# A list-scheduling planner for a two-layer encoder: its DMA transfers served first in, first out, with new service times and tails

## The chip, the cores and the metric

The kernel runs on one core of a Trainium2 chip. The metric is device time in microseconds (us) of one execution. A core has five engines with in-order instruction queues: TensorE (PE in the rows, PEld for its weight loads), VectorE (DVE), ScalarE (ACT), GpSimd (POOL) and SyncE (SP). SP issues every transfer of this kernel; 16 DMA engines carry them.

## The reference, cut to what matters

A trunk of two layers runs over two groups of rows, x_prompt (512 x 1024) and x_sample (1024 x 1024), with shared weights:

```python
def even_layer(x, ...):                      # layer 0
    h = rms_norm(x, norm_g)
    qa, ka, va, qb, kb, vb, gate = split(h @ w_in)
    oa = gqa_attention(axial_rope(rms_norm(qa)), axial_rope(rms_norm(ka)), va)    # 8 query heads, 2 key heads
    ob = rms_norm(diff_attention(partial_rope(..qb), partial_rope(..kb), vb, lam)) * (1 - lambda_init)
    return x + (concat(oa, ob) * silu(gate)) @ w_out

def odd_layer(x, ...):                       # layer 1
    q, k, v, gate = split(rms_norm(x, norm_g) @ w_in)
    o = dilated_attention(q, k, v)           # 16 heads, patterns (128,1), (512,4), (2048,16), merged by softmax weights
    return x + (o * silu(gate)) @ w_out
```

Outputs are y_prompt and y_sample, in float32.

## The kernel before, in words

**Number format.** An operand of a matmul is held as two fp16 halves (high and low), and each product is made in three passes (PASSES: high x high, high x low, low x high).

**Units and granules.** The 1024 rows of w_in and w_out are handled in blocks of 128 output columns. Layer 0 has four units of grouped attention (A) and four of differential attention (B); layer 1 has eight dilated units (C). A unit works on three granules of 512 rows: gi 0 is the prompt, gi 1 and 2 are the sample. For a granule it projects keys and values (kv_piece), queries and gate (qg_piece), makes scores (tile S, L771, L1121, L1169, L1174), takes the exponential, splits the probabilities in two halves (tile h, L795 and L799), has them transposed by DMA (t<-h, L358), and multiplies them with the values (L783, called AV below: 24 or 48 small matmuls into a pj tile).

**The start.** Tiles of 128 rows of x are loaded (L1538), squared on ACT (L1544), scaled, and split into halves on ACT and DVE (h_split, L372 to L377). A DMA transpose of 2048 columns (L385) puts each into hT, from which all projections of the layer are made (L491). hT00 belongs to the prompt, hT01 to the sample (8 transposes). ACT also evicts projections from PSUM into tile z (L653, L732) and scales weights (L422, L472).

**Layer 1's merge.** In a C unit the third pattern's result (tile pk) goes to another layout by four small sends (pn<-pk, L1150), which POOL waits for at L1200.

**The order.** No engine's order is found on the chip. Class Plan is a list scheduler that runs in Python while the kernel is built: each stage has an engine, a duration, a priority pos, what it depends on, and buffers (tokens, limited by CAPS) that it acquires and gives back. run() simulates the engines by these durations. Whenever an engine is free it takes the ready stage with the lowest pos whose buffers are free, and emits its instructions then. A transfer is three stages: the issue on SP, a service on a single server called DMA, and a parallel tail on LAT; who depends on the transfer becomes ready after the tail. The durations never reach the chip; they only decide in which order the instructions stand.

```python
    def dma(self, issue, dur, fn, deps=(), acq=(), use=(), pos=None, keep=0, tail=1.0):
        a = self.add("SP", issue, fn, deps, acq, use, pos, keep)
        x = self.add("DMA", dur, None, [a], (), tuple(acq) + tuple(use), pos)
        return self.add("LAT", tail, None, [x], (), tuple(acq) + tuple(use), pos)
```

Of the kernel before, what the change touches and what calls it, by code (L numbers as in the profile page):

```python
# [59 lines left out]
class Plan:  # L60
# [24 lines left out]
    def dma(self, issue, dur, fn, deps=(), acq=(), use=(), pos=None, keep=0, tail=1.0):  # L85
# [6 lines left out]
    def tdma(self, cols, *args, **kw):  # L92

        return self.dma(0.05 + cols * 0.975e-3, cols * 1.45e-3, *args, tail=0.5, **kw)

# [110 lines left out]
T_DMA = 1.85  # L206
# [6 lines left out]
def trunk_kernel(ctx: ExitStack, tc: tile.TileContext, A: dict, outs: list):  # L213
# [77 lines left out]
    def norm_gain(l, deps=()):  # L291
# [9 lines left out]
        ld = dma(ISSUE, T_DMA, f_ld, deps, [tok])  # L301
# [96 lines left out]
    def wprep(w, cols, ih=None, iz=None, kinds=("whl",), deps=(), keep=2):  # L398
# [10 lines left out]
        for i, c0 in enumerate(cols):  # L409
# [5 lines left out]
            ld = dma(ISSUE, T_DMA, f_ld, deps, [rt], keep=keep)  # L415
# [100 lines left out]
    def qk_stages(zb, ztok, evs, e2, tabs, tdep, ti, kind, isq, dst, dst_acq, dst_use, swap, dst_dep=()):  # L516
# [81 lines left out]
        w1 = dma(ISSUE, 0.3, lambda: nc.sync.dma_start(out=swap()[0:64], in_=dst()[64:128]), [s], (), dst_use)  # L598
        w2 = dma(ISSUE, 0.3, lambda: nc.sync.dma_start(out=swap()[64:128], in_=dst()[0:64]), [s], (), dst_use)
# [23 lines left out]
    def kv_piece(u, gi):  # L623
# [4 lines left out]
        for hf in range(2):  # L628
# [44 lines left out]
            if u.kind == "C":  # L673
                for j in range(2):
# [10 lines left out]
                    vc = dma(ISSUE, 0.3, f_vc, [vl, u.vc_open], (), [u.vct[g], u.vtok])  # L685
# [125 lines left out]
    def spill(l, u, gi, dep):  # L811
# [5 lines left out]
        s = dma(ISSUE, 1.0, f, [dep], (), [u.sgtok[gi]])  # L817
# [87 lines left out]
    def att_B(u, gi):  # L905
# [15 lines left out]
        def chain(b, e0, e1, lo0, n, scs_, f4ts, ex, h4t, first):  # L921
# [9 lines left out]
            s = add("POOL", 0.66, f_co, [s], pos=P.pos - 20)  # L931
# [102 lines left out]
        def fin():  # L1034
# [5 lines left out]
            s = add("ACT", 1.1, f_sq, avs[-1:], (), [otok])  # L1040
# [24 lines left out]
    def att_C(u, gi):  # L1065
# [73 lines left out]
        def send():  # L1139
# [4 lines left out]
            s = add("ACT", act(512) + 0.12, f_ev, avs23[-1:], [pkt], [ot23])  # L1144
            ob["sent"] = []
            for j in range(4):
                def f(j=j):
# [46 lines left out]
        def fin():  # L1194
# [65 lines left out]
    def out_tile(l, g, tl, wo, mix_deps, x_deps, finish):  # L1260
# [264 lines left out]
    def l0_h(g, tls, kinds):  # L1525
# [4 lines left out]
        for i, tl in enumerate(tls):  # L1530
# [185 lines left out]
```

## Time and profile before

| | |
|---|---|
| time, median of 3 runs | 1867.0 us (1866.86 to 1868.43) |
| the profiled execution's own time | 1870.77 us |
| its span, first to last instruction | 1868.5 us |
| mean granted TensorE clock | 0.957 |
| PE / PEld busy | 1671.1 us (89%) / 1399.3 us (75%) |
| DVE / ACT / POOL busy | 1345.7 us (72%) / 1211.2 us (65%) / 692.3 us (37%) |
| instructions | 44772, of them 17626 matmuls |

2.3 us of the profiled execution lie outside its span, and it is 3.8 us above the median. Busy time is time in which an engine executes; PE's own idle time is the span less 1671.1 us, 197.4 us.

### The profile page before, as it was taken

The page shows a single profiled execution, that of the slowest core. Times are in us where ns is not written, and L with a number is a line of the kernel's source. Part 1 is how long each engine was busy: PE and PEld are TensorE (multiplying, and loading weights), DVE is VectorE, ACT ScalarE, POOL GpSimd, SP SyncE. Part 2 cuts the span into 40 slices and gives each one's busy share as a digit, 9 for nine tenths or more (in the row PEclk, how much of TensorE's full clock was granted, in tenths as well). Part 3 has the DMA queues.
Part 4 walks back from the last instruction along what each step waited for, and adds up shares of the span by engine and source line. Part 5 has one row for each costly group of instructions (what it writes and reads, how often), then busy time and mean ns, then how long its engine had stood idle before and what let it go on. Part 6 is the DMA issues. An engine that isn't in the chain of part 4 may idle for free.

```text
span 1868.5 us, 44772 instructions
## 1 busy us (share of the span) xinstructions
PE 1671.1 (89%) x17626; PEld 1399.3 (75%) x17626; DVE 1345.7 (72%) x2985; ACT 1211.2 (65%) x2593; POOL 692.3 (37%) x1204
## 2 busy tenths in 40 slices
PE   4598888999998999697899999999999999995998
PEld 3485676778787877476788887878788888874888
DVE  5779888877887878874555777777777777788442
ACT  5559787777776668753434777676767667787320
POOL 3533233343454453422222435353535353433200
PEclk9799999999999999898999999999999999997999
DMA  9778899987464456697985668586768576777993
GB/s 249 156 136 161 161 177 191 156 161 141 88 127 98 84 116 114 124 200 189 219 199 136 120 134 167 108 166 113 164 117 161 113 142 119 153 152 175 218 233 100
DMA packets 788724, 282.06 MB, mean 151 GB/s; under 512 B 647072, under 2 KB 772256, under 8 KB 788512
## 3 DMA queue, kind: packets, MB, share of 16 engines
q1 hardware_dynamic: 788512, 279.19, 72.7%
q8 instruction: 138, 2.26, 0.5%
q14 instruction: 74, 0.61, 0.1%
HBM read 73.92 MB, written 25.17 MB: 53 GB/s over the span
## 4 chain that ended last, share of the span: by engine, by line
PE 46%; DVE 10%; DMA 10%; POOL 6%; ACT 5%; issue 4%; SPq 0%; DVEq 0%; POOLq 0%; ACTq 0%
PE pj L491 35%; DMA t<-h 9%; PE pj L783 4%; PE pj L505 2%; PE S L1121 2%; DVE f L1096 2%; PE S L771 2%; POOL qs L260 1%; DVE h L799 1%; PE S L1169 1%; ACT f L1106 1%; DVE bs L1017 1%; DVE f L934 1%; ACT f L981 1%; DVE t L566 1%
## 5 line engine op out<-in xcount | busy, mean ns | idle before, releaser
L491 PE MATMUL pj<-whl,hT 128*128 128x256 f16 x7680 | 880.8, 275 | 27.3 <-DMA hT<-h 27.0
L491 PEld LDWEIGHTS <-hT 128*128 128x128 f16 x7968 | 780.2, 99 | 142.4 <-DMA hT<-h 31.3
L783 PEld LDWEIGHTS <-t 128*128 128x128 f16 x4992 | 203.5, 101 | 98.3 <-DMA t<-h 85.7
L1106 ACT ACTIVATE f<-f,cs,csc 128x256 f32<-128x256 f32 (+1 forms) x384 | 218.7, 573 | 82.2 <-DVE cs L777 82.1
L491 PEld LDWEIGHTS <-t 128*128 128x128 f16 x2304 | 228.7, 100 | 47.3 <-DMA t<-h 17.8
L799 DVE TENSOR_TENSOR h<-f,h 128x1024 f16<-128x1024 f32 x148 | 199.6, 1352 | 43.5 <-ACT h L795 43.2
L783 PE MATMUL pj<-V,t 128*128 128x64 f16 (+1 forms) x4032 | 180.4, 204 | 47.3 <-DMA t<-h 46.8
L771 PE MATMUL S<-K,q 128*128 128x512 f16 x640 | 168.9, 397 | 51.4 <-ACT f L1023 21.0
L491 PE MATMUL pj<-whl,t 128*128 128x256 f16 x1728 | 200.7, 278 | 15.7 <-DMA t<-h 13.9
L795 ACT ACTIVATE h<-f 128x1024 f16<-128x1024 f32 x168 | 175.8, 1052 | 14.8 <-DMA t<-h 12.5
L534 POOL TENSOR_SCALAR qs<-qs,we 128x8 f32<-128x8 f32 x87 | 43.0, 495 | 340.6 <-DVE qs L528 320.7
L260 POOL TENSOR_TENSOR qs<-qs,mhalf 128x8 f32<-128x8 f32 x87 | 147.6, 1696 | 7.3
L771 PEld LDWEIGHTS <-q 128*128 128x128 f16 x640 | 61.7, 101 | 109.4 <-issue 58.8
L1331 DVE SCALAR_TENSOR_TENSOR f<-pj,os,f 128x256 f32<-128x256 f32 x96 | 42.0, 479 | 108.9 <-PE pj L491 108.4
L853 DVE TENSOR_REDUCE as<-S 128x1 f32<-128x1024 f32 (+1 forms) x80 | 96.4, 1218 | 15.6 <-PE S L771 15.4
L863 ACT ACTIVATE f<-S,as,asc 128x1024 f32<-128x1024 f32 (+1 forms) x96 | 101.7, 1061 | 7.8 <-DVE h L799 4.4
L477 DVE SCALAR_TENSOR_TENSOR whl<-f,wsm,whl 128x1024 f16<-128x1024 f32 x68 | 94.3, 1400 | 6.4 <-ACT whl L472 6.3
L1096 DVE CUSTOM_DVE_ANT_0 f<-S,mask 128x256 f32<-128x256 f32 x192 | 69.7, 421 | 25.3 <-PE S L1169 25.3
L799 POOL TENSOR_TENSOR h<-f,h 128x1024 f16<-128x1024 f32 x20 | 43.4, 2172 | 117.3 <-ACT h L795 104.3
L422 ACT ACTIVATE t<-f 128x1024 bf16<-128x1024 f32 x74 | 77.8, 1052 | 14.0 <-DMA f<-in_w_in_dram 11.3
L1017 DVE TENSOR_REDUCE bs<-S 128x1 f32<-128x1024 f32 x64 | 76.9, 1217 | 13.2 <-PE S L771 13.2
L585 ACT ACTIVATE st<-t 128x512 f16<-128x512 f32 x87 | 54.2, 623 | 48.6 <-DVE t L579 32.1
(250 smaller groups left out, 2715.2 us busy)
## 6 DMA issues: line engine op xcount, KB each, us to landing
f<-in_w_in_dram SPq DMA_DIRECT2D x58, 512.0 KB, 5.4
mixbuf<-sg SPq DMA_DIRECT2D x48, 256.0 KB, 2.8
f<-mixbuf SPq DMA_DIRECT2D x24, 512.0 KB, 5.5
K<-K SPq DMA_DIRECT2D x78, 128.0 KB, 2.8
f<-in_w_out_dram SPq DMA_DIRECT2D x16, 512.0 KB, 5.1
pn<-pk SPq DMA_DIRECT2D x96, 66.0 KB, 2.6
x1buf<-f SPq DMA_DIRECT2D x12, 512.0 KB, 3.6
Vc<-V SPq DMA_DIRECT2D x96, 64.0 KB, 2.4
```

Of the source, the lines that this page charges most:

```text
L260: G.tensor_tensor(y, v, mhalf[:, 0:n], ALU.pow)
L477: stt(out=part(k, 1, i), in0=b[i][:, nk * k:nk * k + nk, :], scalar=sc(), in1=part(k, 0, i), op0=M, op1=SU)
L491: T.matmul(ps, lhs(k, a), wt(k, b), start=(k == 0 and i == 0), stop=(k == 7 and i == 2))
L771: T.matmul(out[:, 512 * i:512 * i + 512], q, u.K[:, st, gi, hk, :], start=(st == 0), stop=(st == 1))
L783: T.matmul(o, t4[:, 8 * a + base + k, :], v(k, b), start=(k == 0 and i == 0), stop=(k == nk - 1 and i == 2))
L795: S_.activation(out=b["hl"][:, 0, :], in_=b["e"], func=AF.Copy)
L799: (G if on_pool else V).tensor_tensor(b["hl"][:, 1, :], b["e"], b["hl"][:, 0, :], SU)
L853: V.tensor_reduce(out=b["s"][:, 0:nh], in_=b["S"].rearrange("p (h k) -> p h k", h=nh), op=ALU.max, axis=AX.X)
L863: S_.activation(out=b["e"][:, w * i:w * i + w], in_=b["S"][:, w * i:w * i + w], func=AF.Exp, bias=b["s"][:, 2 + i:3 + i], scale=u.sc, accu ...
L1017: V.tensor_reduce(out=b["s"][:, c:c + 1], in_=b["S", c], op=ALU.max, axis=AX.X)
L1096: V.tensor_tensor_reduce(out=b["e"][:, w * i:w * i + w], in0=b["S"][:, w * i:w * i + w], in1=mask(x), scale=1.0, scalar=-3.0e38, op0=AD, o ...
L1106: S_.activation(out=b["e"][:, w * i:w * i + w], in_=b["e"][:, w * i:w * i + w], func=AF.Exp, bias=b["s"][:, i:i + 1], scale=u.sc, accum_ou ...
```

## The change

Only the planner's rules and numbers change. The DMA server takes transfers in the order in which they become ready, no longer by pos. The service times become shorter and the tails longer: for a transpose of 2048 columns 2.97 + 0.5 us becomes 1.84 + 1.71 us, for a load 1.85 + 1.0 us becomes 1.3 + 1.9 us (rows) or 1.75 + 1.9 us (columns of a weight). Some stages of POOL and ACT get larger durations, and the four pn sends no longer depend on one another in the plan. Every line behind L203 moves down by one (by two between L1146 and L1152).

```diff
-    def dma(self, issue, dur, fn, deps=(), acq=(), use=(), pos=None, keep=0, tail=1.0):
+    def dma(self, issue, dur, fn, deps=(), acq=(), use=(), pos=None, keep=0, tail=1.25):
...
-        return self.dma(0.05 + cols * 0.975e-3, cols * 1.45e-3, *args, tail=0.5, **kw)
+        return self.dma(0.05 + cols * 0.975e-3, cols * 0.9e-3, *args, tail=1.2 + cols * 0.25e-3, **kw)
...
-                    heapq.heappush(engs[s.eng], (s.pos, s.seq, s))
+                    heapq.heappush(engs[s.eng], (t if s.eng == "DMA" else s.pos, s.seq, s))
...
-T_DMA = 1.85
+T_ROW = dict(dur=1.3, tail=1.9)
+T_COL = dict(dur=1.75, tail=1.9)
...
-            ld = dma(ISSUE, T_DMA, f_ld, (), [xts[i]])
+            ld = dma(ISSUE, fn=f_ld, acq=[xts[i]], **T_ROW)
...
-            ld = dma(ISSUE, T_DMA, f_ld, deps, [rt], keep=keep)
+            ld = dma(ISSUE, fn=f_ld, deps=deps, acq=[rt], keep=keep, **T_COL)
...
-        w1 = dma(ISSUE, 0.3, lambda: nc.sync.dma_start(out=swap()[0:64], in_=dst()[64:128]), [s], (), dst_use)
+        w1 = dma(ISSUE, 0.25, lambda: nc.sync.dma_start(out=swap()[0:64], in_=dst()[64:128]), [s], (), dst_use)
...
-        s = dma(ISSUE, 1.0, f, [dep], (), [u.sgtok[gi]])
+        s = dma(ISSUE, 0.6, f, [dep], (), [u.sgtok[gi]], tail=1.0)
...
-            s = add("ACT", 1.1, f_sq, avs[-1:], (), [otok])
+            s = add("ACT", 1.45, f_sq, avs[-1:], (), [otok])
...
-            s = add("POOL", 3.2 + pool(512), f_ch, [s, u.sg_ready[gi], u.cst], (), [u.sgtok[gi]])
+            s = add("POOL", 3.6 + pool(512), f_ch, [s, u.sg_ready[gi], u.cst], (), [u.sgtok[gi]])
...
+            s = add("NONE", 0.0, None, [s], [pnt])
...
-                ob["sent"].append(dma(ISSUE, 0.3, f, [s, ob["sent"][-1:]], [pnt] if j == 0 else (),
-                                      [pkt] + ([pnt] if j else [])))
+                ob["sent"].append(dma(ISSUE, 0.25, f, [s], (), [pkt, pnt]))
...
-            s = add("POOL", 1.0, f_w, [ob["sent"], avs1[-1:]], (), [pnt])
+            s = add("POOL", 1.4, f_w, [ob["sent"], avs1[-1:]], (), [pnt])
...
-            s = add("POOL", 0.55 + 3 * pool(512), f_p, [s, u.sg_ready[gi]], (), [pnt, u.sgtok[gi]])
+            s = add("POOL", 1.8 + 3 * pool(512), f_p, [s, u.sg_ready[gi]], (), [pnt, u.sgtok[gi]])
...
-        s = add("POOL", 2.0 + 0.15 * n, lambda: h_rms(b["s"], n), sqs)
+        s = add("POOL", 2.4 + 0.3 * n, lambda: h_rms(b["s"], n), sqs)
...
-        st = x1_done[g, tl] = dma(ISSUE, T_DMA, f_st, evs, (), [xt])
+        st = x1_done[g, tl] = dma(ISSUE, 1.05, f_st, evs, (), [xt], tail=1.6)
```

No instruction is added or taken away on any engine; what moves is the order. Three places show how.

ACT at the start of the program, where the prompt's first projections are evicted (z) while the sample's tiles are squared (L1544) and split (L377). Before:

```order
L653 ACTIVATE z0_280<-pj1_192 128x2x2x64
L661 ACTIVATE V1_282<-pj1_192 128x2x128
L653 ACTIVATE z0_280<-pj3_300 128x2x2x64
L661 ACTIVATE V1_282<-pj3_300 128x2x128
L523 ACTIVATE t11_382<-z0_280 128x512
L1544 ACTIVATE t10_427,hs4_174<-t41_113 128x1024
L1544 ACTIVATE t10_430,hs4_429<-t42_115 128x1024
L732 ACTIVATE z1_467<-pj0_355 128x2x2x64
L742 ACTIVATE sg0_474<-pj0_355,hz_475 128x256
L1544 ACTIVATE t10_478,hs4_429<-f42_172 128x1024
L1544 ACTIVATE t10_512,hs4_511<-f43_278 128x1024
L377 ACTIVATE h41_515<-t40_111 128x1024
```

The same rows of ACT's order after the change:

```order
L1545 ACTIVATE t11_246,hs4_227<-f42_181 128x1024
L1545 ACTIVATE t10_252,hs4_251<-f43_198 128x1024
L378 ACTIVATE h41_293<-t40_111 128x1024
L473 ACTIVATE whl1_296<-f40_158,wsm_188 128x8x128
L473 ACTIVATE whl1_296<-f41_170,wsm_188 128x8x128
L654 ACTIVATE z0_307<-pj1_201 128x2x2x64
L662 ACTIVATE V1_309<-pj1_201 128x2x128
L378 ACTIVATE h42_314<-t41_113 128x1024
L378 ACTIVATE h40_393<-t42_118 128x1024
L654 ACTIVATE z0_307<-pj3_316 128x2x2x64
L662 ACTIVATE V1_309<-pj3_316 128x2x128
L524 ACTIVATE t11_433<-z0_307 128x512
```

The squares and the first splits of the sample's tiles stand ahead of the evictions of z, or between them, where they stood behind.

SP, which issues the sample's loads and the transposes into hT01. Before, from the first such transpose's neighbourhood to the last:

```order
L1538 DMA t40_529<-in_x_sample_dram 128x1024
L385 DMA_TRANSPOSE hT01_534<-h41_515 128x16x128
L385 DMA_TRANSPOSE hT01_534<-h42_518 128x16x128
...
L385 DMA_TRANSPOSE hT01_534<-h41_556 128x16x128
L593 DMA_TRANSPOSE q0_678<-st1_634 128x8x128
L414 DMA f41_706<-in_w_in0_dram 128x8x128
L414 DMA f42_709<-in_w_in0_dram 128x8x128
L598 DMA K0_554<-K0_554 64x1024
L599 DMA K0_554<-K0_554 64x1024
L385 DMA_TRANSPOSE hT01_534<-h42_751 128x16x128
L385 DMA_TRANSPOSE hT01_534<-h40_768 128x16x128
```

SP after the change, the same stretch:

```order
L386 DMA_TRANSPOSE hT01_311<-h41_293 128x16x128
L1539 DMA t40_352<-in_x_sample_dram 128x1024
...
L386 DMA_TRANSPOSE hT01_311<-h42_314 128x16x128
L1539 DMA t42_443<-in_x_sample_dram 128x1024
L386 DMA_TRANSPOSE hT01_311<-h40_393 128x16x128
L386 DMA_TRANSPOSE hT01_311<-h41_441 128x16x128
...
L594 DMA_TRANSPOSE K0_598<-st0_569 128x8x128
L386 DMA_TRANSPOSE hT01_311<-h42_637 128x16x128
L386 DMA_TRANSPOSE hT01_311<-h40_640 128x16x128
...
L386 DMA_TRANSPOSE hT01_311<-h41_704 128x16x128
...
L386 DMA_TRANSPOSE hT01_311<-h42_716 128x16x128
L594 DMA_TRANSPOSE q0_803<-st1_762 128x8x128
```

The first sample transpose now stands ahead of the last three sample loads, and all eight stand ahead of the transpose of the first unit's q (L594, tile q0), behind which the last four stood.

PE at the end of layer 1, from the last unit's scores of granule 1 (q1) to the first block of the output projection (L491 with t); each row is the first of a group of like matmuls. Before:

```order
L1121 MATMUL S0_24990<-K1_23554,q1_24982 128x256
...
L1174 MATMUL S1_25083<-K1_23554,q1_24982 128x128
...
L783 MATMUL pj0_25150<-Vc2_24919,t42_25116 128x64
...
L783 MATMUL pj0_25150<-Vc2_24919,t40_25137 128x64
...
L1121 MATMUL S0_25223<-K1_23554,q2_25175 128x256
...
L783 MATMUL pj1_25267<-V0_23306,t41_25184 128x64
...
L1174 MATMUL S0_25293<-K1_23554,q2_25175 128x128
...
L783 MATMUL pj1_25267<-V0_23306,t42_25240 128x64
...
L1174 MATMUL S1_25351<-K1_23554,q2_25175 128x128
...
L783 MATMUL pj0_25396<-Vc2_24919,t40_25368 128x64
...
L491 MATMUL pj2_25445<-whl1_23799,t41_25383 128x256
```

After the change, the same place:

```order
L1122 MATMUL S0_25054<-K1_23553,q1_25014 128x256
...
L1175 MATMUL S1_25132<-K1_23553,q1_25014 128x128
...
L1122 MATMUL S0_25159<-K1_23553,q2_25097 128x256
...
L784 MATMUL pj2_25205<-Vc2_24928,t40_25174 128x64
...
L1175 MATMUL S0_25246<-K1_23553,q2_25097 128x128
...
L784 MATMUL pj2_25205<-Vc2_24928,t41_25243 128x64
...
L1175 MATMUL S1_25297<-K1_23553,q2_25097 128x128
...
L492 MATMUL pj1_25324<-whl1_24002,t42_25268 128x256
...
L784 MATMUL pj0_25399<-V0_23414,t41_25352 128x64
...
L492 MATMUL pj3_25429<-K0_24835,t42_25268 128x256
...
L784 MATMUL pj0_25399<-V0_23414,t41_25427 128x64
```

The first scores of granule 2 now stand ahead of the last AVs of granule 1, and blocks of the output projection stand between the AVs of granule 2.

## Rows read from the trace of the kernel before

**Rows 1.** Stretches of the span: length, busy PE, PEld, DVE, ACT, POOL, clock, DMA share, GB/s.

```profile
0.00:105.00 105.00, 58.39 (x403) 44.54 (x404) 66.88 (x129) 59.38 (x99) 43.06 (x76) 0.84 0.84 196
105.00:350.00 245.00, 212.00 (x2640) 166.02 (x2639) 205.61 (x277) 190.77 (x335) 90.44 (x105) 0.99 0.89 164
350.00:750.00 400.00, 383.26 (x3869) 314.81 (x3867) 322.56 (x522) 293.98 (x604) 175.10 (x313) 0.98 0.63 119
750.00:1000.00 250.00, 209.61 (x1822) 175.25 (x1819) 155.86 (x299) 125.67 (x216) 67.92 (x156) 0.91 0.82 188
1000.00:1650.00 650.00, 624.66 (x7060) 541.31 (x7061) 480.56 (x1444) 449.84 (x1147) 274.21 (x482) 0.98 0.68 135
1650.00:1760.00 110.00, 82.41 (x907) 67.58 (x906) 79.70 (x223) 73.42 (x172) 36.51 (x62) 0.84 0.85 185
...
53.62:99.91 46.29, 26.87 (x162) 18.91 (x162) 32.49 (x50) 27.16 (x49) 20.34 (x36) 0.71 0.86 181
...
1691.45:1729.73 38.28, 20.36 (x220) 15.02 (x220) 31.21 (x109) 31.86 (x80) 10.91 (x24) 0.63 0.85 185
```

**Rows 2.** Waits of PE, 0 to 105 us: line, releaser, us in total, times, longest.

```profile
PE pj L491 <- DMA hT<-h: 27.0, 8, 10.1
```

**Rows 3.** PE's timeline at the start: start, us, line, count, [idle before].

```profile
60.12 8.29 PE L491 MATMUL pj<-whl,hT 128*128 128x256 f16 x48 [6.50 <-DMA hT<-h]
...
99.91 15.88 PE L491 MATMUL pj<-whl,hT 128*128 128x256 f16 x144
...
129.21 2.78 PE L491 MATMUL pj<-whl,hT 128*128 128x256 f16 x24
```

**Rows 4.** ACT's timeline, 26 to 60 us, with the same columns.

```profile
35.61 0.38 ACT L653 ACTIVATE z<-pj 128x256 f32<-128x256 f32 x1 [4.82 <-PE pj L491]
...
43.18 0.38 ACT L653 ACTIVATE z<-pj 128x256 f32<-128x256 f32 x1 [6.91 <-PE pj L491]
...
51.30 1.99 ACT L377 ACTIVATE h<-t 128x1024 f16<-128x1024 f32 x2
```

**Rows 5.** SP's timeline, 0 to 100 us, with the same columns.

```profile
54.01 6.64 SPq L385 DMA_TRANSPOSE hT<-h  x2
...
86.51 9.23 SPq L385 DMA_TRANSPOSE hT<-h  x4
```

**Rows 6.** Tile hT, from the transposes' issue to their landing.

```profile
DMA to landing us min/median/max: 4.3/5.7/7.7
```

**Rows 7.** Waits of PE, 105 to 350 us.

```profile
PE S L771 <- ACT f L863: 19.3, 18, 1.9
PE pj L783 <- DMA t<-h: 10.9, 12, 2.6
```

**Rows 8.** AV matmuls (L783) alone, 105 to 350 us: busy PE, PEld.

```profile
105.00:350.00 245.00, 49.47 (x1368) 46.68 (x1368) 0.99 0.89 164
```

**Rows 9.** Waits of PE, 750 to 1000 us.

```profile
PE S L771 <- ACT f L1023: 14.9, 6, 5.4
```

**Rows 10.** Waits of PE, 1000 to 1650 us.

```profile
PE pj L783 <- DMA t<-h: 22.6, 15, 2.8
```

**Rows 11.** SP's timeline, 1660 to 1760 us: the first and last of one granule's pn sends.

```profile
1666.38 0.61 SPq L1150 DMA_DIRECT2D pn<-pk  x1
...
1678.22 0.73 SPq L1150 DMA_DIRECT2D pn<-pk  x1
```

**Rows 12.** PE's timeline at the end of layer 1.

```profile
1691.45 3.85 PE L1121 MATMUL S<-K,q 128*128 128x256 f16 x16 [4.88 <-DMA q<-st]
...
1698.08 0.82 PE L1169 MATMUL S<-K,q 128*128 128x256 f16 x6
1704.71 1.46 PE L783 MATMUL pj<-Vc,t 128*128 128x64 f16 x24 [5.82 <-DMA t<-h]
1709.02 1.46 PE L783 MATMUL pj<-Vc,t 128*128 128x64 f16 x24 [2.85 <-DMA t<-h]
...
1726.56 1.46 PE L783 MATMUL pj<-Vc,t 128*128 128x64 f16 x24 [4.51 <-DMA t<-h]
```

More of the change, by code (lines that the diff above doesn't have):

```diff
@@ L300, in f_ld @@
             nc.sync.dma_start(out=b["g"], in_=A[f"norm{l}"].unsqueeze(0).to_broadcast([128, D]))
-        ld = dma(ISSUE, T_DMA, f_ld, deps, [tok])
+        ld = dma(ISSUE, fn=f_ld, deps=deps, acq=[tok], **T_ROW)
         def f_g():
@@ L597, in qk_stages @@
             return [s]
-        w1 = dma(ISSUE, 0.3, lambda: nc.sync.dma_start(out=swap()[0:64], in_=dst()[64:128]), [s], (), dst_use)
-        w2 = dma(ISSUE, 0.3, lambda: nc.sync.dma_start(out=swap()[64:128], in_=dst()[0:64]), [s], (), dst_use)
+        w1 = dma(ISSUE, 0.25, lambda: nc.sync.dma_start(out=swap()[0:64], in_=dst()[64:128]), [s], (), dst_use)
+        w2 = dma(ISSUE, 0.25, lambda: nc.sync.dma_start(out=swap()[64:128], in_=dst()[0:64]), [s], (), dst_use)
         return [s, w1, w2]
@@ L684, in kv_piece @@
                         u.vc_open = add("NONE", 0.0, None, [vl, u.tdep], [u.vct[g]])
-                    vc = dma(ISSUE, 0.3, f_vc, [vl, u.vc_open], (), [u.vct[g], u.vtok])
+                    vc = dma(ISSUE, 0.25, f_vc, [vl, u.vc_open], (), [u.vct[g], u.vtok])
                     u.vc_ready.setdefault(g, []).append(vc)
@@ L930, in f_co @@
                 G.tensor_scalar(out=x[:, 9:10], in0=x[:, 6:7], scalar1=box["clam"], scalar2=0.0, op0=M, op1=AD)
-            s = add("POOL", 0.66, f_co, [s], pos=P.pos - 20)
+            s = add("POOL", 0.9, f_co, [s], pos=P.pos - 20)
             def f_cm():
@@ L1268, in f_ld @@
             nc.sync.dma_start(out=b["mt"], in_=mixbuf[l][row:row + 128, :])
-        s = dma(ISSUE, T_DMA, f_ld, mix_deps, [rt], keep=2)
+        s = dma(ISSUE, fn=f_ld, deps=mix_deps, acq=[rt], keep=2, **T_ROW)
         box["lastld"] = s
@@ L1308, in f_x @@
                     nc.sync.dma_start(out=x, in_=x1buf[row - 64:row + 64, :])
-        sx = dma(ISSUE, T_DMA, f_x, [x_deps, sl], [xt], keep=1)
+        sx = dma(ISSUE, fn=f_x, deps=[x_deps, sl], acq=[xt], keep=1, **T_ROW)
         evs, mms = [], []
@@ L1592, in fin0 @@
         s = add("ACT", act(1024, 1), f_sq, evs, [t1t], [xt])
-        s = add("POOL", 2.2, lambda: h_rms(b["s"], 1), [s])
+        s = add("POOL", 2.8, lambda: h_rms(b["s"], 1), [s])
         hs1.append(h_split(1, g, tl, x, xt, lambda: b["s"][:, 1:2], [s, st], [proj_mm[0, g]]))
@@ L1641, in f_st @@
                 nc.sync.dma_start(out=dst[128 * tl - 64:128 * tl + 64, :], in_=x())
-        dma(ISSUE, T_DMA, f_st, evs, (), [xt])
+        dma(ISSUE, 1.05, f_st, evs, (), [xt], tail=0.9)
     layer(1, units1, w1, lambda: box["ih", 1], A["w_out1"],
```

## The prediction

> **What bounds the kernel now.** I read the stages first. In [rows 1] PE's idle time is the length of a stretch less its busy time: 46.6 us in the first 105 us, 33.0 in the A stage (105 to 350), 16.7 in B (350 to 750), 40.4 in the passage to layer 1 (750 to 1000), 25.3 in layer 1 up to 1650, 27.6 at its end. PE is the engine that works most in every stage, so the time moves only where one of these idle times moves. In A the cover is thin: DVE is busy 205.61 of 245 us and ACT 190.77.
>
> Then I asked what ends PE's waits. At the start it is the transposes into hT, 27.0 us in eight waits [rows 2]. PE runs dry at 53.62 us (60.12 less the wait of 6.50) and has no wait again from 99.91 on [rows 3]. In these 46.29 us it is busy 26.87, at a granted clock of 0.71, so it idles 19.4 [rows 1]. The reason stands on SP: the first sample transposes are issued at 54.01 and the last four only from 86.51 to 95.74 [rows 5], and they take 5.7 us to land [rows 6]. SP is late because ACT is: it stands 4.82 and 6.91 us in front of two evictions of z, and splits the sample's first tiles only at 51.30 [rows 4].
>
> In A PE waits 19.3 us for ACT to give a score buffer back and 10.9 us for transposed probabilities [rows 7]; in the passage 14.9 us for ACT [rows 9]; in layer 1 22.6 us for transposed probabilities [rows 10]. At the end of layer 1 single AVs wait up to 5.82 us [rows 12].
>
> **The start.** The change adds no instruction, so each term is a wait that moves. In ACT's new order two squares, one split and two weight scalings stand ahead of the first eviction of z. They fit in the 4.82 us that ACT stands idle there and a few more; a split takes 1.0 us (1.99 for two, [rows 4]). The first sample transpose can then be issued near 37 us, 17 us earlier. The eight need 2.3 us of SP each (9.23 / 4, [rows 5]), 18.5 in all, and share SP with three loads that wait for buffers of earlier tiles; at about 4.3 us from one to the next the last is issued near 68 and lands near 74, where it now lands at 99 (93.4 + 5.7). If nothing else held PE, the stretch of 46.29 us would shrink by its whole idle time, 19.4, and by some 8 us of the 26.87 that it is busy, since 48 matmuls take 8.29 us in it and 24 take 2.78 behind it [rows 3]: -27 is the far end. The near end is -6.5, the first wait alone. I take -20, because the last transposes still come only just ahead of the projections that read them: some waits of 1 to 3 us remain. The two squares move the first eviction of z back; its next reader is the norm of K, and in the new order the first score stands behind 52.6 us of PE's priced work (prices below) instead of 31.7, which hides it. Without that cover it would cost about 3 us, three rows of 1.0.
>
> **The A stage.** Here the change can cost. I counted in PE's order the work between the last score of a block and the AV that needs it, with a projection matmul at 0.110 us (15.88 / 144, [rows 3]), an AV matmul at 0.036 (49.47 / 1368, [rows 8]) and scores at 0.24 (3.85 / 16, [rows 12]). Its mean over the A stage falls from 17.3 to 14.8 us, so every AV stands 2.5 us closer to its score. Twelve of the 57 AVs (1368 / 24, [rows 8]) wait already. If each of them waits 2.5 us longer, that is +30. But a later AV lets ACT finish, and PE's 19.3 us for score buffers [rows 7] lie in the same loop; what one wait takes the other gives back, and +30 less 19.3 is about +11. If the transposes' new places on SP make them land earlier, the 10.9 us go and nothing comes, so the bounds are -11 and +30. I take +10.
>
> **B and the passage.** B keeps its order of scores and AVs nearly as it was: 0. In the passage the output projection begins after 651.5 us of priced work instead of 648.4, and PE's waits are for ACT, whose work is the same: 0, with bounds of 8 us either way (half of the 14.9 us of [rows 9]).
>
> **Layer 1.** The least work between scores and AV grows from 10.6 to 12.0 us. Fifteen waits of 1.5 us each [rows 10] would all but go at -1.4 each, -20 in all. Against it, the four pn sends of a granule, now spread over 11.8 us on SP with transposes between them [rows 11], come one right behind another: 4 x 0.6 us that a transpose behind them can be late; if all fifteen waits grow by a fourth of that, 0.6 us each, +9. What a transpose waits for on SP is mostly other transposes, which stay; so I take -5, nearer to nothing. The sends' earlier end helps POOL, which is off the path.
>
> **The end of layer 1.** From 1691.45 to 1729.73 PE is busy 20.36 of 38.28 us at a clock of 0.63 [rows 1]: 17.9 idle, and 4.88 before it for q [rows 12]. The AVs stand right behind their scores: the score that ends at 1698.90 has its AV at 1709.02, 10.1 us later, with hardly any work between [rows 12]. After the change granule 2's first scores stand between granule 1's scores and its AVs, and blocks of the output projection between granule 2's AVs; only two short distances are left in the new order, 4.4 and 5.1 us of priced work. With a latency of 9 us they wait 4.6 and 3.9, 8.5 in all; the wait for q I keep whole. So 22.8 becomes 13.4, -9.4, and five AVs at 0.87 us instead of 1.46 (36.2 ns x 24 from [rows 8] against [rows 12]) give 3 more. I take -12; bounds 0 (the new places wait as much) and -18 (only the wait for q stays).
>
> **Sum.** -20 + 10 + 0 - 5 - 12 = -27: the profiled execution's 1870.8 us become 1843.8, and as it stands 3.8 us above the median of the runs, the forecast is 1840.
>
> **The rivals.** *The start's gain is given back in A.* DVE and ACT have 39 and 54 us of slack there, and PE that arrives 20 us earlier meets the same DVE work. With A at +25: -20 + 25 - 5 - 12 = -12, 1855. For it: the waits for ACT. Against: DVE and ACT are not full.
>
> *Slower: the AVs stand too close to their scores.* Its place is the A stage, its price the further wait of each of the 57 AVs. It decides from 0.54 us each, beyond my +10, since 57 x 0.54 = 31 eats the 27 and the 3.7 that a measurement can tell. At 1 us each the sum is -27 + 57 = +30, 1897. For it: the transposes into hT land in 4.3 to 7.7 us [rows 6], a spread of 3.4, wider than the 2.5 us taken away, while the planner now reckons with one service and one tail for all. Against: now only 12 of 57 wait, 0.9 us each.
>
> The Trainium skill, DMA: Bandwidth & Descriptors, Queues, rings and completion order, says that transfers are consumed in ring order but that completion is not FIFO per issuing engine, so the new queue of the plan would be no truer than the old. By that rule the spread stays unplanned and the time is that of this rival, 1897; the trace agrees on the spread (3.4 us) and shows no overtaking.
>
> *Nothing.* The orders differ, but if the weight tiles, not hT, held PE at the start, and the end kept its waits, A's +10 would meet -5 and -6: 1866. Against: 27.0 of the 46.6 us that PE idles there are waits for hT [rows 1, 2].
>
> *More.* Start -27, A 0, layer 1 -20, end -18: -65, 1802.
>
> **How the numbers follow.** A measurement of this kernel can tell about 0.2%, 3.7 us, from no change. Forecast, 1822 to 1853: 0.55. Given back in A, 1853 to 1863: 0.17. Within 1863.3 to 1870.7: 0.07. Slower: 0.16. More, below 1822: 0.05. Faster is 0.55 + 0.17 + 0.05 = 0.77. The range reaches from 1820 to 1871, which leaves out the slower case and most of the last, 0.2; the forecast's own range is 1822 to 1853.
>
> **What would show it.** Right: the last sample transpose is issued before 75 us and PE passes its first 105 us with 20 us less idle time; the waits of L784 in A grow by no more than 20 us; between the last scores and the output projection no AV waits more than 5 us; pn sends stand in fours. Wrong: L784's waits in A above 40 us; the first transposes into hT01 still behind 50 us; layer 1's steady waits above 30 us.

## The result and the profile after

The changed kernel takes 1855.5 us (median of 4 runs, 1854.6 to 1858.6), the kernel before 1867.7 (4 runs): a ratio of 0.9932, interval [0.9911, 0.9953]. The sign was right and the time lies in the wide range (1820 to 1871), but outside the forecast's own (1822 to 1853): the gain is 12.3 us where 27 were forecast. The profiled execution took 1854.62 us (span 1852.4), 16.1 us less than that of before, which lay 3 us above its median; the terms below are measured between the two profiled executions and sum to that 16.1.

The stretches of the span after the change, with the columns of [rows 1]:

```profile
0.00:105.00 105.00, 72.13 (x572) 59.15 (x573) 78.27 (x162) 61.52 (x108) 57.05 (x95) 0.95 0.91 209
105.00:350.00 245.00, 213.31 (x2675) 163.40 (x2673) 205.12 (x269) 205.92 (x359) 81.05 (x88) 0.95 0.96 174
...
750.00:1000.00 250.00, 216.78 (x1917) 181.02 (x1915) 151.94 (x308) 126.62 (x219) 58.97 (x150) 0.91 0.87 196
1000.00:1650.00 650.00, 624.05 (x7072) 538.79 (x7070) 482.25 (x1460) 452.40 (x1159) 284.95 (x493) 0.99 0.68 136
1650.00:1760.00 110.00, 83.26 (x871) 69.04 (x866) 67.42 (x198) 62.95 (x143) 31.66 (x51) 0.83 0.82 178
```

In the first 105 us PE is busy 13.7 us more than in [rows 1], and its clock is 0.95 instead of 0.84. In A (105 to 350) the clock is 0.95 instead of 0.99. In layer 1 (1000 to 1650) and at its end PE's busy times are those of before within 1 us, and so are its idle times: no waiting was taken out there.

PE's waits after the change: first 0 to 105 us, then 105 to 350, then 1000 to 1650.

```profile
PE pj L492 <- DMA hT<-h: 21.2, 9, 10.2
...
PE pj L784 <- DMA t<-h: 20.4, 18, 2.5
PE S L772 <- ACT f L864: 10.6, 8, 2.3
...
PE pj L784 <- DMA t<-h: 14.8, 18, 3.2
```

Against [rows 7] the AVs in A wait 9.5 us more and the scores 8.7 us less: the trade that the prediction spoke of. Against [rows 10] the AVs in layer 1 wait 7.8 us less, but the time there did not fall.

SP's timeline at the start, after the change:

```profile
37.75 5.14 SPq L386 DMA_TRANSPOSE hT<-h  x1
...
53.35 5.91 SPq L386 DMA_TRANSPOSE hT<-h  x2
...
62.74 4.95 SPq L386 DMA_TRANSPOSE hT<-h  x2
...
72.85 4.54 SPq L386 DMA_TRANSPOSE hT<-h  x1
```

The first sample transpose is issued at 37.75 instead of 54.01, the last at 72.85 instead of after 90 [rows 5]. PE then runs through:

```profile
56.20 9.70 PE L492 MATMUL pj<-whl,hT 128*128 128x256 f16 x72 [1.93 <-DMA hT<-h]
...
79.64 14.94 PE L492 MATMUL pj<-whl,hT 128*128 128x256 f16 x120 [2.71 <-DMA hT<-h]
```

The wait of 6.50 [rows 3] has become 1.93. PE at the end of layer 1:

```profile
1670.64 0.58 PE L433 MATMUL pj<-wsm,ones 128*128 128x1 f32 x2 [4.74 <-ACT t L423]
1675.64 1.46 PE L784 MATMUL pj<-V,t 128*128 128x64 f16 x24 [4.41 <-DMA t<-h]
1676.91 3.85 PE L1122 MATMUL S<-K,q 128*128 128x256 f16 x16
...
1685.66 2.00 PE L1122 MATMUL S<-K,q 128*128 128x256 f16 x8 [2.14 <-DVE m L1097]
1690.12 2.01 PE L1122 MATMUL S<-K,q 128*128 128x256 f16 x8 [2.45 <-DVE m L1097]
...
1696.98 0.59 PE L1175 MATMUL S<-K,q 128*128 128x128 f16 x4 [3.57 <-DVE md L1097]
...
1704.51 7.43 PE L492 MATMUL pj<-whl,t 128*128 128x256 f16 x48 [1.64 <-DMA t<-h]
...
1736.14 6.99 PE L492 MATMUL pj<-whl,t 128*128 128x256 f16 x48 [2.18 <-DMA t<-h]
...
1762.02 3.27 PE L492 MATMUL pj<-whl,t 128*128 128x256 f16 x20 [2.47 <-DMA t<-h]
```

The AV waits of [rows 12] are gone between the scores, but PE now waits in front of them (4.74 for the square of a weight tile, 4.41 for an AV), in them (2.14, 2.45, 3.57 for DVE to give score buffers back) and in the output projection (2.18, 2.47).

**PE's place, stage by stage.** Both kernels issue the same matmuls, so I compare the times at which PE has done the same amount of work: the matmuls in their order, each at the rate of an undisturbed run (0.109 us for a projection), 1553 us in all. "At 325" is the point where 325 us of that work lie behind. The difference to before, in us (negative is earlier):

| work done | 75 | 100 | 325 (A ends) | 625 (B ends) | 825 (layer 1 begins) | 1400 | 1553 |
|---|---|---|---|---|---|---|---|
| changed kernel | -18.9 | -22.1 | -11.5 | -16.3 | -19.4 | -19.4 | -16.1 |

So the start gave 19 to 22 (up to the point 100: 16.5 us less waiting, 5.7 less busy time), A took 11 back, B and the passage gave 8, layer 1 nothing, and the end took 3. The start (up to 100) and the end (from 1400) in both, before first, with the columns of [rows 1]:

```profile
0.00:168.40 168.40, 115.59 (x1039) 90.28 (x1040) 120.49 (x229) 104.53 (x179) 70.78 (x114) 0.90 0.79 175
0.00:146.20 146.20, 109.93 (x1024) 88.34 (x1025) 114.36 (x217) 97.61 (x170) 71.90 (x113) 0.96 0.91 196
1669.60:1868.50 198.90, 166.12 (x1643) 143.66 (x1641) 96.28 (x272) 76.24 (x162) 31.56 (x56) 0.91 0.76 181
1650.30:1852.40 202.10, 168.64 (x1628) 144.65 (x1624) 94.85 (x271) 75.28 (x157) 34.01 (x53) 0.90 0.73 173
```

How far one execution can be trusted is seen from six runs below that have the same order up to 1400 (e6_notend, h0_pool to h2_pool, h3_dve7, h4_act7): at 100 they lie 21.4 to 23.3 us ahead of before, at 325 6.3 to 10.8, at 825 12.7 to 21.1. With the changed kernel the seven lose 10.6 to 15.1 us in A, 13 in the mean.

### The profile page after: what moved, and what is told of

It is laid out like the page before. It is cut to its first block, busy times and chain, and to the rows that moved or that the text cites. A ratio compares the mean times of both kernels' runs of the same rounds, so it can differ in the third digit from the quotient of the medians.

```text
span 1852.4 us, 44798 instructions
## 1 busy us (share of the span) xinstructions
PE 1675.0 (90%) x17626; PEld 1398.4 (75%) x17626; DVE 1332.2 (72%) x2985; ACT 1212.8 (65%) x2593; POOL 695.5 (38%) x1204
## 3 DMA queue, kind: packets, MB, share of 16 engines
q8 instruction: 138, 2.26, 0.5%
## 5 line engine op out<-in xcount | busy, mean ns | idle before, releaser
L492 PE MATMUL pj<-whl,hT 128*128 128x256 f16 x7680 | 882.3, 275 | 22.2 <-DMA hT<-h 21.2
L492 PEld LDWEIGHTS <-hT 128*128 128x128 f16 x7968 | 782.8, 99 | 145.6 <-DMA hT<-h 23.1
L492 PEld LDWEIGHTS <-t 128*128 128x128 f16 x2304 | 228.9, 100 | 40.0 <-DMA t<-h 9.8
L800 DVE TENSOR_TENSOR h<-f,h 128x1024 f16<-128x1024 f32 x148 | 187.7, 1273 | 57.4 <-ACT h L796 55.0
L492 PE MATMUL pj<-whl,t 128*128 128x256 f16 x1728 | 202.4, 279 | 8.2 <-DMA t<-h 8.2
L478 DVE SCALAR_TENSOR_TENSOR whl<-f,wsm,whl 128x1024 f16<-128x1024 f32 x68 | 87.7, 1305 | 8.2 <-ACT whl L473 8.2
L473 ACT ACTIVATE whl<-f,wsm 128x1024 f16<-128x1024 f32 x68 | 75.8, 1140 | 16.8 <-PE pj L492 14.3
L1122 PE MATMUL S<-K,q 128*128 128x256 f16 (+1 forms) x384 | 79.3, 371 | 4.6 <-DVE m L1097 4.6
```

The lines of the kernel that those rows point to most:

```text
L478: stt(out=part(k, 1, i), in0=b[i][:, nk * k:nk * k + nk, :], scalar=sc(), in1=part(k, 0, i), op0=M, op1=SU)
L492: T.matmul(ps, lhs(k, a), wt(k, b), start=(k == 0 and i == 0), stop=(k == 7 and i == 2))
L800: (G if on_pool else V).tensor_tensor(b["hl"][:, 1, :], b["e"], b["hl"][:, 0, :], SU)
L1122: T.matmul(s[:, L * i:L * i + L], q, k, start=(sk == 0), stop=(sk == 1))
```

## The experiments

The theory of the prediction: A takes time back because its AVs stand closer to their scores, and the end gains because AVs no longer stand right behind theirs. The rivals: whoever comes to A early gives it back in any order, and the end has one length in any order. Each row below is the difference to before at the same work, as in the table above, with the medians of the timed runs; "before" is that of the same chip.

| run | 100 | 325 | 625 | 825 | 1400 | 1553 | median | ratio [interval] |
|---|---|---|---|---|---|---|---|---|
| e1_fifo | -9.1 | -13.6 | -15.0 | -31.7 | -38.0 | -39.9 | 1831.0 | 0.980 [0.978, 0.982] |
| e2_dma | -14.4 | -9.3 | -10.6 | -14.8 | -24.9 | -25.7 | 1844.5 | 0.987 [0.985, 0.989] |
| e4_start | -22.1 | -9.0 | -10.8 | -13.5 | -16.7 | -15.0 | 1855.1 | 0.993 [0.991, 0.995] |
| e5_notA | -21.3 | -7.0 | -11.8 | -13.1 | -12.6 | -13.3 | 1855.5 | 0.993 [0.992, 0.995] |
| f1_fifo_dma | -14.7 | -8.3 | -10.4 | -21.0 | -35.4 | -36.5 | 1840.1 | 0.986 [0.983, 0.989] |
| f2_fifo_costs | -8.7 | -12.6 | -17.0 | -27.6 | -35.7 | -37.6 | 1833.4 | 0.982 [0.980, 0.984] |
| f3_fifo_pn | -7.6 | -11.5 | -12.3 | -26.1 | -35.5 | -36.0 | 1831.1 | 0.979 [0.977, 0.982] |
| g1_dve | -21.0 | +11.6 | +5.2 | +1.4 | -0.2 | -0.1 | 1867.8 | 1.001 [0.999, 1.003] |
| g2_act | -23.4 | -7.5 | -11.6 | -15.0 | -14.3 | -13.0 | 1856.4 | 0.993 [0.990, 0.995] |
| g3_dma | -22.2 | -6.2 | -11.7 | -16.1 | -18.3 | -21.8 | 1857.0 | 0.995 [0.992, 0.997] |
| g5_low | -22.6 | -14.7 | -20.6 | -22.0 | -16.6 | -13.6 | 1847.6 | 0.988 [0.985, 0.990] |
| m1_fifo_pool | -9.5 | +0.6 | +0.4 | -15.4 | -21.7 | -23.7 | 1841.5 | 0.985 [0.983, 0.988] |

The differences are of the one profiled execution, which can lie up to 9 us beside the median of its runs (g5_low, g3_dma).

### The parts of the change

**The queue rule alone**, on the kernel before:

```diff
-                    heapq.heappush(engs[s.eng], (s.pos, s.seq, s))
+                    heapq.heappush(engs[s.eng], (t if s.eng == "DMA" else s.pos, s.seq, s))
```

> Only the queue rule: the planner's DMA server takes transfers first in, first out, with every number of the kernel before. The order already shows the first sample transposes ahead of the last three sample loads, and the distance from scores to AV in the A stage stays at 17.2 us of priced work (16.7 before, 14.7 after the whole change). Theory (the loss in A comes from AVs that stand closer to their scores): the start gains 15 to 22 us and A keeps it, so about 18 us faster than before. Rival (whoever arrives in A early meets the same busy DVE and ACT, and gives about 10 us back): about 8 us faster.

Measured: 36.7 us faster, three times the whole change, twice what the theory said and over four times what the rival said. The start gives less than half of what the change gives, A takes nothing back, and 17 us come from the passage (625 to 825): for the same work PE waits 30.7 us there instead of 41.3, and is busy 214.9 instead of 221.0, at a clock of 0.94 instead of 0.91 (before, then e1_fifo).

```profile
753.00:1015.20 262.20, 220.91 (x1924) 184.99 (x1922) 160.87 (x311) 130.14 (x223) 69.25 (x158) 0.91 0.81 186
737.90:983.50 245.60, 214.94 (x1926) 181.84 (x1924) 164.87 (x321) 133.31 (x227) 67.43 (x160) 0.94 0.89 202
```

PE's waits for transposes from 750 to 1000 us before, beside [rows 9]:

```profile
PE pj L491 <- DMA t<-h: 11.0, 3, 7.8
PE pj L783 <- DMA t<-h: 9.5, 5, 3.0
```

and the large waits of e1_fifo in the same stretch of time:

```profile
PE S L796 <- ACT f L1048: 12.8, 5, 5.4
PE pj L516 <- DMA t<-h: 7.2, 2, 5.4
PE pj L808 <- DMA t<-h: 3.2, 1, 3.2
```

The wait for ACT is nearly that of [rows 9]; the waits for transposes, of the output projection and of the AVs, fell from 20.5 to 10.4 us.

**The DMA numbers alone** (services and tails as in the change, the queue by pos):

> Only the DMA numbers (shorter services, longer tails), with the queue still served by pos. The distance in A falls to 15.1 us, nearly as after the whole change (14.7). Theory (distance): the start gains about 20 us, A gives about 8 back, so about 12 us faster than before. Rival (early arrival): the same 20 and 10, so this run does not tell the two apart by itself; against the run with the queue rule alone it does, which by the theory is about 8 us better in A and by the rival equal.

23 us faster: again more than the whole change.

**Both, without the new costs and with the chained sends**:

> The queue rule and the DMA numbers together, without the new costs of POOL and ACT and with the sends of pn still in a chain. The queue rule alone gave 37 us, the DMA numbers alone 23, the whole change 12. If the new costs and the sends are what takes 25 us of the queue rule's gain, this run is 30 to 40 us faster than before. If the queue rule and the DMA numbers spoil each other, it is 10 to 20 us faster, like the whole change.

27.5 us faster, between the two cases that were expected. **The queue rule with the pn sends of the change, and with the new costs of POOL and ACT**:

> The queue rule with the pn sends that no longer depend on one another, no other number changed. The queue rule alone gave 37 us, queue rule and DMA numbers 27, all together 12. If the sends in a row are what costs in layer 1 (a transpose behind four of them is late), this run is 25 to 32 us faster than before; if the new costs of POOL and ACT are it, 34 to 40.

> The queue rule with the new costs of POOL and ACT, the old DMA numbers and the old chain of sends. The queue rule alone gave 37 us, with the DMA numbers 27, with the sends 36 to 39, the whole change 12. If the new costs take back the gain by themselves, this run is 18 to 25 us faster than before; if only together with the DMA numbers, 32 to 40.

Against the kernel before on the same chips (1870.8 and 1868.1) these are 39.7 and 34.7 us faster, so neither the sends nor the costs take much by themselves. Queue rule, DMA numbers and the rest together lose 15 us against f1_fifo_dma, most of it between 825 and 1400, in layer 1, where the change stands still and f1_fifo_dma gains 14 (PE waits 17.5 us there instead of the change's 26.0 and is busy 6 us less). The sends and the costs were not run singly on top of f1_fifo_dma, so which of them does it, and by which order, stays open.

### What takes the start's gain back in A

The planner's rules were made to depend on its own time:

```diff
+RULES = {
+    "F": lambda now: now < 105.0,
+    "D": lambda now: now < 105.0,
+    "C": lambda now: now < 105.0,
+}
...
-                heapq.heappush(events, (now + s.dur, 1, s.seq, s))
+                heapq.heappush(events, (now + at(s.dur, now), 1, s.seq, s))
```

F is the queue rule, D the DMA numbers, C the costs of POOL and ACT; at() gives the old or the new number. 

> All new numbers and the new queue, but only for the first 105 us of the plan; behind that the planner goes back to the rules of before. Distance in A 17.5 us. Theory (distance): PE stands 20 to 22 us ahead at the end of the start and still about 20 at 350 us; the whole is 18 to 22 us faster than before. Rival (early arrival): 22 ahead at the start, 11 at 350 us, the whole about 11 us faster.

e5_notA has the condition `not 105.0 <= now < 385.0`. 

> The new rules everywhere except from 105 to 385 us of the plan (the A stage), where the rules of before hold; the sends of pn as in the change. Distance in A 17.5 us. Theory (distance): the 10.6 us that A lost stay, so about 22 to 26 us faster than before. Rival (early arrival): as the whole change, about 12 to 16 us faster.

Both came out as the rival said. With the old rules in A, and the AVs as far from their scores as before (17.5 us of priced work), A takes 13.1 and 14.3 us back, as much as the 13 of the changed order. The orders of the table's first seven rows and that of the change come to A's end 7.0 to 13.6 us ahead, whether they entered it 8 or 22 ahead. The closer AVs are not the cause.

What PE does in A shows in the same work, from 100 to 325, with the columns of [rows 1]: before, the change, e1_fifo, f1_fifo_dma, and g5_low, which comes below.

```profile
168.40:432.80 264.40, 233.02 (x2970) 185.24 (x2969) 218.41 (x272) 210.19 (x372) 96.48 (x106) 0.99 0.93 169
146.20:421.30 275.10, 240.42 (x2985) 187.06 (x2984) 220.51 (x285) 217.78 (x381) 95.28 (x107) 0.96 0.91 165
159.30:419.20 259.90, 231.38 (x2984) 183.43 (x2982) 216.84 (x273) 212.71 (x376) 97.72 (x106) 1.00 0.97 172
153.60:424.50 270.90, 233.45 (x2969) 183.54 (x2967) 221.69 (x282) 215.66 (x378) 92.36 (x107) 0.99 0.91 165
145.80:418.10 272.30, 240.09 (x2986) 186.61 (x2985) 185.69 (x284) 216.90 (x382) 89.61 (x107) 0.96 0.92 167
```

Of the 10.7 us that the change loses in A, 7.4 are busy time of PE, for the same work at a clock of 0.96 instead of 0.99, and only 3.3 are waiting. In e4_start they are 6.1 and 7.1 (clock 0.97), in e5_notA 8.4 and 6.0 (0.96); e1_fifo, which loses nothing, has 1.00. The sum of the waits does not set the clock by itself: f1_fifo_dma waits 37.4 us there, more than the change, and keeps 0.99. Why the clock falls in the other orders is not shown.

Then single engines got more work in A, on the changed kernel. DVE:

```diff
             (G if on_pool else V).tensor_tensor(b["hl"][:, 1, :], b["e"], b["hl"][:, 0, :], SU)
+            if u.kind == "A" and not on_pool:
+                box["twice"] = box.get("twice", 0) + 1
+                if box["twice"] % 2 == 0:
+                    V.tensor_tensor(b["hl"][:, 1, :], b["e"], b["hl"][:, 0, :], SU)
```

> The changed kernel with every second low half of the probabilities in the A units computed twice on DVE (the same result again), some 24 extra instructions of about 1.25 us, 30 us of DVE work, nearly all ahead of the middle of the kernel; the planner does not know of them. If DVE's work sets the pace of the A stage (and so took back what the start gained), the time at the end of A and of the whole grows by 20 to 30 us. If ACT or the DMA engines set it, by less than 8 us.

ACT, the copy of every third high half repeated:

> The changed kernel with every third high half of the probabilities in the A units copied twice on ACT, some 24 extra instructions of about 1.05 us, 25 us of ACT work. If ACT sets the pace of A, the whole grows by 17 to 25 us; if DVE or the DMA engines do, by less than 7 us.

The DMA engines:

```diff
+            if u.kind == "A":
+                for m in (mixbuf[1][row:row + 512, u.f0:u.f0 + 128], x1buf[row:row + 512, u.f0:u.f0 + 128]):
+                    nc.sync.dma_start(out=m.rearrange("(t p) f -> p t f", p=128), in_=u.sg[gi])
```

> The changed kernel with each of the twelve spills of the A units stored two times more, to places that are overwritten later: 24 stores of 256 KB, at the 174 GB/s of the A stage about 36 us of the DMA engines' time and 14 us of SP. If the DMA engines (0.96 busy in A after the change) set the pace of A, the whole grows by 20 to 36 us; if DVE or ACT do, by less than 8 us.

ACT and the DMA engines took it in: -7.5 and -6.2 at A's end lie within the spread of the seven runs of the same order or at its edge. DVE did not. Its rows of g1_dve for 0 to 460 us (line, form, count, busy, mean, idle before):

```profile
L800 DVE TENSOR_TENSOR h<-f,h 128x1024 f16<-128x1024 f32 x60 | 72.7, 1218 | 10.9 <-ACT h L796 9.4 <-issue 1.4
L804 DVE TENSOR_TENSOR h<-f,h 128x1024 f16<-128x1024 f32 x29 | 39.1, 1350 | 1.0
```

39.1 us more of DVE move A's end by about 20 us, from between -11.5 and -6.3 to +11.6. If DVE's load were also what takes the start's gain, less of it should give the gain back. In g5_low the 60 low halves are left out (written as zero), in m1_fifo_pool, which stands on e1_fifo, half of them go to POOL instead of about a quarter:

```diff
-            (G if on_pool else V).tensor_tensor(b["hl"][:, 1, :], b["e"], b["hl"][:, 0, :], SU)
+            if u.kind == "A" and not on_pool:
+                ts(out=b["hl"][:, 1, :], in0=b["hl"][:, 0, :], scalar1=0.0, scalar2=None, op0=M)
+            else:
+                (G if on_pool else V).tensor_tensor(b["hl"][:, 1, :], b["e"], b["hl"][:, 0, :], SU)
```

> The changed kernel with the low halves of the probabilities that DVE makes in the A units left out (written as zero from the fp16 high half, so that the instruction stays and gets shorter): some 48 instructions of 1.22 us become shorter by perhaps half or more, 30 us or so off DVE without anything on POOL. If DVE's work sets the pace of A (30 us more of it cost 23 us), A ends 10 to 20 us earlier than in the changed kernel. If A hangs on a wait that DVE's load does not set, by less than 5.

In m1_fifo_pool, a part of one line:

```diff
-on_pool=len(avs) % APOOL == 2
+on_pool=len(avs) % 2 == 1
```

> The queue rule alone, as in the run that gave 37 us, and in the A units every second low half of the probabilities on POOL instead of about every fourth: some 20 operations of 1.25 us go from DVE to POOL, where one takes 2.2. If DVE's work sets the pace of A (30 us more of it cost 23 us at the end of A), taking 25 us away gives 10 to 19 us there and most of it at the end: 1812 to 1822. If not, or if POOL's slower operation makes its AVs late, 1828 to 1840.

The low halves in g5_low, 0 to 460 us:

```profile
L801 DVE TENSOR_SCALAR h<-h 128x1024 f16<-128x1024 f16 x60 | 27.7, 468 | 22.7 <-ACT h L796 22.7
```

Of the changed kernel's time on them 47 us are gone (60 at 1.25 us are 74.4), and A ends at -14.7, 3 us ahead of the best of the seven; the whole is 8 us faster by the medians (1847.6 against 1855.5, on another chip). More DVE work costs half a us a us, less of it frees a tenth. PE's stretch of A shows why: g5_low waits 32.2 us there, as the kernel before does (31.4), and the 7.1 us by which it is still longer busy come with the clock of 0.96. g1_dve waits 48.1 us and is busy 248.9, at 0.94. So DVE's load bears on the waits, which without it are those of before, but the larger part of what the change loses in A is the clock. m1_fifo_pool ends A 14 us later than e1_fifo and is 10 us slower in all, just beyond its second case (the last section shows what DVE does in it).

### The end of layer 1

The rules of the change up to 1500 us of the plan, those of before behind it (`now < 1500.0`):

> The whole change up to 1500 us of the plan, and the rules of before behind that, so that only the end of layer 1 is ordered as before. My prediction's step (the new order takes 12 us of AV waits out of the end): this run is about 12 us slower than the changed kernel, 1867. Rival (the end lasts the same in every order, 178 to 183 us from the last projection to the last matmul in all six orders seen so far, since the merge, the spill and the reload set it): within 4 us of the changed kernel, 1852 to 1860.

1857.0, ratio 0.994 [0.991, 0.996]: the rival's number. From 1400 on it takes 203.6 us, the change 202.1, the kernel before 198.9; other runs lie between 195.3 and 201.7, so the 3 us of the end are within the spread. The rival's reason, that merge, spill and reload set the end's length, is tested below. PE's times from the last projection (the last L491 or L492 with hT) on, in us:

| kernel | first block of the output projection | fifth block (first of the sample) | last matmul |
|---|---|---|---|
| before | 44.2 | 94.3 | 178.3 |
| changed | 39.5 | 97.0 | 182.7 |
| e1_fifo | 42.2 | 93.7 | 177.7 |
| e6_notend | 44.4 | 94.9 | 178.9 |
| f3_fifo_pn | 40.6 | 92.4 | 176.4 |
| h0_pool, h1_pool, h2_pool | 43.1, 39.1, 39.4 | 98.2, 96.3, 97.1 | 182.3, 180.3, 181.1 |
| h3_dve7, h4_act7 | 41.6, 42.1 | 98.1, 97.0 | 182.1, 181.0 |

From the fifth block on the last matmul follows 84 to 86 us later in all of them: PE has hardly a wait there. To find what sets the fifth block's start, work was added to the last unit of the changed kernel: 30 small POOL operations in the merge of one granule (0, 1 or 2; they take 8 to 11 us of POOL),

```diff
                 G.tensor_tensor(dd[:, 0], m1, pn[:, :, 128:130], SU)
+                if u.f0 == 896 and gi == 0:
+                    dj = small(8, "dj", 1).rearrange("p (t h) -> p t h", h=2)
+                    for _ in range(30):
+                        G.tensor_tensor(dj, m1, dd[:, 0], SU)
```

> The changed kernel with 30 small extra operations on POOL (about 6 us, into a tile that nothing reads) in the merge of the last unit's granule 0, the prompt, ahead of its spill. POOL is little used there, so only what hangs on that merge moves. If the end hangs on the way from the prompt's last AV over merge, spill and reload to the first block of the output projection, the whole grows by 4 to 7 us; if it hangs on the later granules or on AVs and their scores, by less than 2.

> The changed kernel with 30 small extra operations on POOL (about 6 us) in the merge of the last unit's granule 1, the first half of the sample. In fourteen orders the first block of the output projection for the sample starts 92 to 98 us after the last projection, and PE has no wait behind it; if that start hangs on granule 1's merge, spill and reload, it moves by 4 to 7 us and the whole with it. If not, less than 2, as with granules 0 and 2.

> The same 30 extra operations on POOL in the merge of the last unit's granule 2, the last rows of the sample. If the end hangs on the last granule's merge, the whole grows by 4 to 7 us; if the output projection's blocks of the other rows hide it, by less than 2.

and the low or the high halves of the unit's probabilities made twice (the line that makes them put in a loop `for _ in range(2 if u.l == 1 and u.f0 == 896 else 1)`):

> The changed kernel with every low half of the probabilities in the last unit of layer 1 computed twice on DVE, fourteen extra instructions of about 1.25 us, 17 us. If the end hangs on the softmax of the last granules on DVE, the way from the last projection to the last matmul grows from 183 us by 6 us or more; if it hangs on the projection's own blocks and their transposes, by less than 3.

> The changed kernel with every high half of the probabilities in the last unit of layer 1 copied twice on ACT, fourteen extra instructions of about 1.05 us, 15 us. If the end hangs on ACT, which works without a pause from 1682 to 1693 us there, it grows by 6 us or more; else by less than 3.

Medians 1851.7, 1850.0, 1850.1 (two runs each), 1859.8 and 1856.9 against 1855.5, and the way from the last projection to the last matmul does not grow in any of them. POOL's merges, DVE and ACT have room at the end; none of them sets its length. What does stays open; no run made the transposes there later.

## Why the prediction was wrong

**The start (-20): right, in size and mechanism.** 18.9 to 22.1 measured; the first sample transpose comes at 37.75 us (37 forecast), the last is issued at 72.85 (68), and the waits that remain are of 0.3 to 2.7 us. The idle time of the first 105 us fell by 13.7 us where the prediction's sign asked for 20; part of the gain is the clock instead.

**The A stage (+10): the size about right, 10.6 to 15, but by luck, and the mechanism wrong.** I derived it from AVs that stand 2.5 us closer to their scores. The waits did move as described, but the AVs' 9.5 us more and the scores' 8.7 us less all but cancel; e4_start and e5_notA keep the old distance and lose 13 to 14; and 7.4 of the 10.7 us are no wait but matmuls at a lower clock, a term that the prediction did not have. The rival "the start's gain is given back in A" named the right place. Of its two engines DVE counts when work is added, ACT does not, and taking work from DVE gives little.

**B and the passage (0): -4.8 and -3.1**, the second inside its bounds. The queue rule alone gains 17 in the passage, which the prediction had not seen: it named only the waits for ACT there and left those for transposes, 20.5 us, out.

**Layer 1 (-5): 0.** The AV waits fell by 7.8 us and the time did not: other waits of the same stretch grew from 4.2 to 11.0 us. The sends in fours cost nothing measurable on the queue rule alone (f3_fifo_pn).

**The end (-12): +3. This is the step that failed most.** The prediction took the stretch 1691.45 to 1729.73, counted which waits the new order removes, and let everything behind it come earlier by the sum. The waits did go: from the first scores of granule 1 to the first block PE needs 27.6 us instead of 38.3, -10.7 against -9.4 forecast. But the scores begin 11.9 us behind the last projection instead of 5.9, because a sum over the squares of a weight tile and an AV now stand right ahead of them, and from the first block to the fifth PE needs 57.5 us instead of 50.1. Over the whole end (1400 to 1553) PE waits 33.5 us instead of 32.8. The 3 us for faster AVs did not come either: three of them still take 1.46 us. With the order of before in that place (e6_notend) the stretch and the kernel's time are the same within their spread. The bound 0, "the new places wait as much", is what was measured, within 3 us; I chose near the other.

**The rivals.** "Given back in A" has 1855 beside it, and 1855.5 was measured. That is luck: its A was +25 and 11 were measured, its end -12 and +3 were measured. Slower by late AVs: the further wait is 9.5 us in all, 0.17 us for each of 57 AVs, far from the 0.54 at which it decides. The rule of the Trainium skill weighed there (DMA: Bandwidth & Descriptors, Queues, rings and completion order: completion is not FIFO per issuing engine) did not decide this case: after the change the transposes into hT land in 4.3 to 8.9 us, the spread is still there, and yet the plan with a first-in-first-out queue alone is the fastest of all runs (1831.0).

## What to carry to other kernels

A wait that goes away is worth what the next fixed point behind it allows: at the end, 10.7 us were taken out of one stretch and came back ahead of it and behind it. Before summing waits in a window, ask at which later point PE has not waited in either order, and compare the distance to that point. Split what a stage loses into waiting and busy time: in A most of the loss was busy time at a lower clock, which no list of waits shows. A planner's rules do not add up: one of the four parts of this change alone (the queue rule, 1831.0 us, 0.980 [0.978, 0.982]) is three times the whole, so each part of such a change should be run alone before all are taken.

## What the runs showed of the hardware

Work that goes from DVE to POOL made the rest of DVE slower. Two of DVE's rows from 105 to 350 us, in e1_fifo:

```profile
L824 DVE TENSOR_TENSOR h<-f,h 128x1024 f16<-128x1024 f32 x45 | 56.2, 1254 | 13.5 <-ACT h L820 13.0 <-issue 0.5
L583 DVE TENSOR_TENSOR t<-t,qs 128x512 f32<-128x512 f32 x10 | 9.9, 993 | 0.2
```

and in m1_fifo_pool, where POOL has 28 of the low halves at 2.26 us each:

```profile
L824 DVE TENSOR_TENSOR h<-f,h 128x1024 f16<-128x1024 f32 x27 | 39.0, 1449 | 23.8 <-ACT h L820 20.1 <-issue 3.7
L583 DVE TENSOR_TENSOR t<-t,qs 128x512 f32<-128x512 f32 x10 | 15.8, 1580 | 0.2
```

The same instructions take 1.45 instead of 1.25 us and 1.58 instead of 0.99 on DVE while POOL works more (e1_fifo has 14 low halves on POOL in that stretch). The timeline shows how, here from 203 us of m1_fifo_pool:

```profile
203.10 3.11 POOL L824 TENSOR_TENSOR h<-f,h 128x1024 f16<-128x1024 f32 x1
204.14 2.61 DVE L583 TENSOR_TENSOR t<-t,qs 128x512 f32<-128x512 f32 x1
```

Five of the ten of L583 meet no low half on POOL and take 0.68 us. The other five start while one runs, 1.4 to 2.1 us before its end, and take 2.00 to 2.61 us: each is longer by the rest of POOL's instruction, less 0.13 us. The low halves on DVE (L824) do the same: 1.22 us alone, up to 2.89 us, and longer by the rest of POOL's instruction, less 0.14 us, wherever one was running with more than that left. So in this trace neither of the two ends before a low half that POOL has begun: they wait for it. The maxima over the scores (L878) take 1.22 us in both runs, whatever POOL does.

So part of what left DVE came back as longer DVE instructions, and a low half takes 2.26 us on POOL; that is why I take m1_fifo_pool's loss against e1_fifo to come from the move itself, but no run parts the two. And at the start the clock is won with the waits: 0.95 instead of 0.84 in the first 105 us, where PE idles 14 us less; there the 120 projections from 79.64 on run at 0.124 us each, against 0.173 for 48 of them in [rows 3].
